# Router by token halves, with column-group products and split residual seeds, in a one-core encoder block with a mixture of experts

## Chip, cores and metric

One of the eight cores of a Trainium2 chip runs the whole program in one launch. The metric is the device time of one execution in microseconds (us), given as the median of several executions. Engines are called by the profile's names: PE (matrix products), PEld (its weight loads), DVE (vector), ACT (scalar and table functions), POOL, and SP, which here only issues DMAs.

## The reference, cut to what matters

An encoder layer over 256 tokens of width 1024: three mixing branches, a gated sum, an output projection with a residual, then a hierarchical mixture of 16 experts, and a final norm. The change touches the output projection, the norm after it, the router and the gathering of tokens for the first group of experts.

```python
x = x + (g_ret * y_ret + g_na * y_na + g_xa * y_xa) @ w_out[l]
x = x + _hierarchical_moe(_rmsnorm(x, g_ffn[l]), w_router_group[l], ...)

# in _hierarchical_moe, t = (256, 1024) normed tokens
grp_p = softmax(t @ w_rg + b_rg)                  # 4 groups
grp_w, grp_idx = top_k(grp_p, 1)
exp_logits = (t @ w_re + b_re).reshape(-1, 4, 4)  # 4 experts in each group
in_grp = exp_logits of the chosen group
top_w, top_idx = top_k(softmax(in_grp), 2)        # 2 of the 4
top_w = top_w / sum(top_w) * grp_w
for g in range(4):
    a, u = t @ w_gate[g], t @ w_up[g]             # 4 experts, width 512
    out += (silu(a) * u * combine[:, g]) @ w_down[g]
```

## The kernel before, in words

Up to the mixed branch outputs the program is ordered by a planner. From the third output of the last branch on, it runs under `manual_schedule()`: every engine executes in the order in which the Python code emits, so the order of the calls is the order on each queue.

**The tail before the experts.** `wout(q, pts)` multiplies a quarter (two blocks of 128 rows) of `w_out`, split in a high and a low part, with the mixed tokens `m_hi`, `m_lo`: 6 products of 128x512 for each of the two token halves `a` (128 tokens each). Four quarters fill the column half n=0 (into `p0`), four more n=1 (into `p1`). `x1_sum(n, a)` (L889) adds the residual on DVE; `x1_sq` (L893) takes the sum of squares on ACT; `x1_T` (L898) transposes four 128x128 blocks on PE, `x1_ev` (L901) copies them to SBUF on ACT; `logits(n, a)` (L906) is four products with the transposed token block as the stationary operand and the router's weights `wr` (32 columns, 20 of them used) as the moving one. Each such fp32 product is two passes on PE, and the profile counts passes. `x1_rstd(a)` (L957, L958) gives the norm's factor `r2`, with a power on POOL. `normed_hi` (L985, ACT) and `normed_lo` (L989, DVE) write the normed tokens, split in two parts. `seed` (L912) puts x1 itself into the four accumulators `acc` by a product with the identity, so that the experts' outputs are added on top.

**Routing.** `route(a)` (L1017 on) is a chain of eleven steps of small DVE instructions, from the logits with factor and bias (L1018) over two maxima with their indices to the mask `msk` (L1010). The chains of the two halves are interleaved on DVE. The products at L1060 with a triangular and an all-ones matrix count for each token its place within its expert; L1073 adds that to `posm`, `counts` (L1077) takes the largest count, and `select(0)` (L1114) compares `posm` with 0..63, which gives the 0/1 matrices `pd` (tile X) that gather tokens into 64 slots for each of the 4 experts of group 0. `gather(pd, lead=True)` (L1129) multiplies the normed high parts with `pd` (16 products of 128x256), then the low parts (16 more), and the evictions at L1152 (ACT) and L1156 (DVE) write `xg`.

**Experts.** For each of 8 pairs of experts: gate and up (`gate_up`, L1197), down (`down`, L1216), and the scatter back into `acc` (L1254). In these products the stationary operand has 64 columns, and two column groups of PE (outputs on partitions 0 to 63 and 64 to 127) are written by products in turn. L1169 and L1176 (`place`) prepare the scatter.

**Loads of the expert weights.** `plan` is a list of 96 loads of 1 MB each (gate and up as two DMAs of 512 KB, down as one of 1 MB) in the order of their use. `fetch(tag)` (issues at L152, on SP's queue) takes the next load of the list into a buffer that has come free; SP waits there until the buffer's last reader is done. Counted from 0, the loads 0 to 11 are issued up to 291 us. Loads 12 and 13 go into the buffers of the w_out quarters 0 and 1 of n=1 (in tile h), load 14 into A0 (the mixed tokens of rows 0 to 511), 15 and 16 into the buffers of quarters 2 and 3, 17 into E0 (mixed tokens of rows 512 to 1023), 18 and 19 into T0 and T1, whose space is freed with the temporary pools after the last logits. From load 20 on, each goes into a buffer that the experts themselves give back: load 20 goes into B after the first `gate_up` quarter. The list and the buffers are as many after the change as before.

**PSUM.** Four banks of pool `psa` (tile pj) hold `p0`, `p1`, then transposes, then `acc`; four of `psc` (tile b) hold the logits, transposes, counts and gathers.

Of the kernel before, what the change touches and what calls it, by code (L numbers as in the profile page):

```python
# [9 lines left out]
F32 = mybir.dt.float32  # L10
# [20 lines left out]
def hybrid_encoder_kernel(  # L31
# [162 lines left out]
    def pj(shape):  # L194
        return psa.tile(shape, F32, tag="pj", name=nm("pj"))
# [677 lines left out]

    def wout(q, pts):
        w = halves.pop(0)
        for a in range(2):
            ts = slice(a * P, (a + 1) * P)
            for k in range(2):
                kk = 2 * q + k
                PE.matmul(pts[a], m_hi[kk // 4][:, kk % 4, ts], w[k][0], start=kk == 0, stop=False)  # L880
                PE.matmul(pts[a], m_hi[kk // 4][:, kk % 4, ts], w[k][1], start=False, stop=False)
                PE.matmul(pts[a], m_lo[kk // 4][:, kk % 4, ts], w[k][0], start=False, stop=kk == KT - 1)
        if not parts:
            hl_tags.remove(w[2])
            fetch(w[2])

# [16 lines left out]
    def logits(n, a):  # L903
        for j in range(4):
            k = 4 * n + j
            PE.matmul(rlog[a], x1T[n][:, j, a * P : (a + 1) * P], wr[:, k], start=k == 0, stop=k == KT - 1)  # L906

    acc = [[None, None], [None, None]]

    def seed(base, a, n):  # L910
        acc[a][n] = acc[a][n] or pj([P, 512])
        PE.matmul(acc[a][n], ident, base[:, a, n * 512 : n * 512 + 512], start=True, stop=False)  # L912

    x1 = slot("C1", [P, 2, D])
    p0 = [pj([P, 512]) for _ in range(2)]
    for q in range(4):
        if q < 2:
            mt = mixed_T(1, q)
        wout(q, p0)
        if q < 2:  # L920
            mixed(1, q, mt)
        feed()
    psx.close()
# [4 lines left out]

    rlog = [bank([P, 32]) for _ in range(2)]
    p1 = [pj([P, 512]) for _ in range(2)]  # L930
    xt = [bank([P, 4, P]) for _ in range(2)]
    x1T[0] = tmp([P, 4, 256])
    x1_sum(0, 0, p0)
    x1_sum(0, 1, p0)
    x1_sq(0, 0)
    x1_sq(0, 1)
    wout(0, p1)
    feed()
    wout(1, p1)
    fetch("A0")  # L940
    x1_T(0, 0, xt[0])
    x1_T(0, 1, xt[1])
    feed()
    x1_ev(0, 0, xt[0])
    x1_ev(0, 1, xt[1])
    wout(2, p1)
    logits(0, 0)
    logits(0, 1)
    feed()
    wout(3, p1)  # L950
    xt = [pj([P, 4, P]) for _ in range(2)]
    x1T[1] = tmp([P, 4, 256])
    r2 = cp.tile([P, 2], F32, name="r2")

    def x1_rstd(a):
        v = tiny(1, tag="var")
        V.scalar_tensor_tensor(v, ss4[:, 2 * a : 2 * a + 1], 1e-6, ss4[:, 2 * a + 1 : 2 * a + 2], op0=ALU.add, op1=ALU.add)  # L957
        G.tensor_tensor(r2[:, a : a + 1], v, nhalf[:, :1], op=ALU.pow)  # L958

    x1_sum(1, 0, p1)  # L960
    fetch("E0")
    x1_T(1, 0, xt[0])
    x1_sq(1, 0)
    x1_ev(1, 0, xt[0])
    x1_sum(1, 1, p1)
    x1_rstd(0)
    x1_T(1, 1, xt[1])
    logits(1, 0)
    x1_sq(1, 1)
    x1_ev(1, 1, xt[1])  # L970
    logits(1, 1)
    x1_rstd(1)
    tx.close()
    tpx.close()
    fp = ctx.enter_context(tc.tile_pool(name="fp", bufs=1))
    for tag in ("T0", "T1"):
        home[tag] = fp
        fetch(tag)

# [12 lines left out]

    for a in range(2):
        for n in range(2):
            normed_hi(a, n)
            seed(x1, a, n)
    show("x1", x1)
    gval = cp.tile([P, 2, 8], F32, name="gval")
# [18 lines left out]
    def route(a):  # L1017
        V.scalar_tensor_tensor(lgt[:, a, 0:20], rlog[a][:, :20], r2[:, a : a + 1], rb, op0=ALU.mult, op1=ALU.add)  # L1018
        yield
        V.max(gval[:, a], lgt[:, a, 16:24])  # L1020
        yield
        V.max_index(gidx[:, a], gval[:, a], lgt[:, a, 16:24])
        yield
        V.tensor_tensor(ohg[:, a], io4, gidx[:, a, 0:1].to_broadcast([P, 4]), op=ALU.is_equal)
        yield
        V.tensor_tensor(
            sel[:, a],
            lgt[:, a, 0:16].rearrange("p (g e) -> p g e", g=4),
            ohg[:, a].unsqueeze(2).to_broadcast([P, 4, 4]),
            op=ALU.mult,  # L1030
        )
        yield
        V.tensor_reduce(pad[:, a, 0:4], sel[:, a].rearrange("p g e -> p e g"), axis=AX.X, op=ALU.add)
        yield
        V.max(eval_[:, a], pad[:, a])
        yield
        V.max_index(eidx[:, a], eval_[:, a], pad[:, a])
        yield
        for i in range(2):
            V.tensor_tensor(oh[:, i, a], io4, eidx[:, a, i : i + 1].to_broadcast([P, 4]), op=ALU.is_equal)  # L1040
        yield
        V.tensor_add(m4[:, a], oh[:, 0, a], oh[:, 1, a])
        yield
        spread(msk, m4, a)
        yield

    rt = [route(a) for a in range(2)]
    for i in range(16):
        if i < 11:
            next(rt[0])  # L1050
        if i >= 5:
            next(rt[1])
    pp = bank([P, 3, 16])
    for o, pieces in (
        (pp[:, 0], ((tri, 0),)),
        (pp[:, 1], ((tri, 1), (ones, 0))),
        (pp[:, 2], ((ones, 0), (ones, 1))),
    ):
        for i, (l, a) in enumerate(pieces):
            PE.matmul(o, l, msk[:, a], start=i == 0, stop=i == len(pieces) - 1)  # L1060
    posm = cp.tile([P, 2, 16], F32, name="posm")
    V.tensor_scalar(posm, msk, 1e6, -1e6, op0=ALU.mult, op1=ALU.add)
    gneg = tiny(2, tag="gneg")
    V.tensor_scalar_mul(gneg, gval[:, :, 0], -1.0)
    gsum = tiny(2, tag="gsum")
    for a in range(2):
        gex = tiny(4, tag="gex")
        A.activation(gex, lgt[:, a, 16:20], AF.Exp, bias=gneg[:, a : a + 1], accum_out=gsum[:, a : a + 1])
    e21 = tiny(2, tag="e21")
    V.tensor_sub(e21, eval_[:, :, 1], eval_[:, :, 0])  # L1070
    A.activation(e21, e21, AF.Exp)
    A.activation(warm, e21[:, 0:1], AF.Silu)
    V.tensor_add(posm, posm, pp[:, 0:2])  # L1073
    cmax = tiny(1, tag="cmax")

    def counts():
        V.tensor_reduce(cmax, pp[:, 2], axis=AX.X, op=ALU.max)  # L1077

    def weights():
# [28 lines left out]

    counts()

    def select(g):
        pd = slot("X", [P, 2, 4, SLOTS], F32R)
        for a in range(2):
            V.tensor_tensor(  # L1114
                pd[:, a],
                posm[:, a, 4 * g : 4 * g + 4].unsqueeze(2).to_broadcast([P, 4, SLOTS]),
                iota.unsqueeze(1).to_broadcast([P, 4, SLOTS]),
                op=ALU.is_equal,
            )
        return pd  # L1120

    def gather(pd, lead=False):
        pts = [bank([P, 2, 256]) for _ in range(4)]

        def part(u, x, first):
            for j in range(2):
                ks = slice((2 * u + j) * P, (2 * u + j + 1) * P)
                for a in range(2):
                    PE.matmul(  # L1129
                        pts[u][:, j],  # L1130
                        x[:, a, ks],
                        pd[:, a].rearrange("p e s -> p (e s)"),
                        start=first and j + a == 0,
                        stop=not first and j + a == 2,
                    )

        if lead:
            for u in range(4):
                part(u, x1_hi, True)
            for n in range(2):  # L1140
                for a in range(2):
                    normed_lo(a, n)
        xg = slot("C1", [P, KT, 4, SLOTS])
        for u in range(4):
            pt = pts[u]
            if not lead:
                part(u, x1_hi, True)
            part(u, x1_lo, False)
            if u % 2:
# [12 lines left out]
        return xg  # L1162
# [128 lines left out]

    def experts(pd, first, lead=False):
        st = {}
# [17 lines left out]

        xg = gather(pd, lead)
        for p in range(NP):
            tail = p == NP - 1
# [31 lines left out]

    pd0 = select(0)
    experts(pd0, weights, True)
    run.close()

# [81 lines left out]
```

## Time and profile before

| | us |
|---|---|
| median of 3 executions | 544.58 (544.51 to 544.82) |
| the profiled execution, whole | 544.12 |
| its span, first to last instruction | 542.2 |
| PE busy | 527.7 (97% of the span) |
| DVE busy | 263.6 (49%) |
| ACT busy | 228.6 (42%) |
| DMA queue of the loads | 158.80 MB, 80.4% of 16 engines |

The profile page gives busy time by engine, slices of the span, DMA queues, groups of instructions by source line (L906 is line 906 of the kernel), and the DMA issues. The timeline lists instructions in order of time; neighbours of one kind are merged (x8), and the duration is then that of the merged stretch. The duration of a PE row runs to a modelled end, and passes overlap in the array: the rate of a stretch is read from the distance of the starts. In brackets stands the idle time of the engine before the row and what ended it.

### The profile page before, as it was taken

The numbers are of one execution on the slowest core, as the hardware profiler recorded it, in microseconds if no ns is written. First come the engines' busy times: TensorE is split into PE (matmuls) and PEld (weight loads), VectorE is DVE, ScalarE is ACT, GpSimd is POOL, SyncE is SP. The second block draws the span as 40 slices with busy tenths as digits, with TensorE's granted clock in tenths as the row PEclk, the third lists the DMA queues.
The fourth block names the chain that finished last, engine by engine and source line by source line (L and its number), as shares of the span: only waits on it lengthen the run. The fifth ranks groups of instructions, "written<-read, shape, count | busy, mean of one in ns | idle before, by whom it ended". The sixth has DMA issues, their size and how long they took to land. (4 is left out here: it accounts for less than half of the span.)

```text
span 542.2 us, 7482 instructions
## 1 busy us (share of the span) xinstructions
PE 527.7 (97%) x2912; PEld 360.0 (66%) x2912; DVE 263.6 (49%) x461; ACT 228.6 (42%) x378; POOL 18.2 (3%) x21
## 2 busy tenths in 40 slices
PE   8999999999999999999999999999999999999992
PEld 7999899976778888888888863353435343534340
DVE  6688898985657768384566161030112111210122
ACT  7684567697754464544435251111111111111123
POOL 0014000040000000000000000000000000000000
PEclk9999999999999999999999999999999999999997
DMA  8997878044446698739983789999999999999962
GB/s 302 390 328 224 244 142 257 14 158 152 154 147 208 239 328 279 280 107 403 351 315 143 289 332 342 414 406 417 406 415 409 410 413 407 417 405 418 406 245 82
DMA packets 89815, 159.91 MB, mean 295 GB/s; under 512 B 13104, under 2 KB 27824, under 8 KB 89776
## 3 DMA queue, kind: packets, MB, share of 16 engines
q1 hardware_dynamic: 89056, 158.80, 80.4%
q10 hardware_dynamic: 720, 0.58, 0.3%
q8 instruction: 25, 0.41, 0.3%
q14 instruction: 14, 0.11, 0.1%
HBM read 158.32 MB, written 1.05 MB: 294 GB/s over the span
## 5 line engine op out<-in xcount | busy, mean ns | idle before, releaser
L129 DVE TENSOR_TENSOR h<-r,h 128x1024 fp32r<-128x1024 f32 x58 | 70.1, 1222 | 28.4 <-ACT h L128 28.1
L128 ACT CAST h<-r 128x1024 fp32r<-128x1024 f32 x58 | 59.9, 1047 | 17.7 <-PE pj L308 11.5
L306 PE MATMUL pj<-h,A 128*128 128x512 f32 x160 | 63.2, 395 | 0.0
L308 PE MATMUL pj<-h,A 128*128 128x512 f32 x160 | 62.6, 391 | 0.0
L307 PE MATMUL pj<-h,A 128*128 128x512 f32 x160 | 62.5, 391 | 0.0
L1205 DVE TENSOR_TENSOR gs<-gs,b 64x512 f32<-64x512 f32 x16 | 11.0, 691 | 87.1 <-ACT gs L1204 87.1
L288 PE MATMUL pj<-A,h 128*128 128x256 f32 x160 | 45.7, 286 | 0.0
L290 PE MATMUL pj<-A,h 128*128 128x256 f32 x160 | 45.5, 284 | 0.0
L289 PE MATMUL pj<-A,h 128*128 128x256 f32 x160 | 45.3, 283 | 0.0
L306 PEld LDWEIGHTS pj<-h,A 128*128 128x128 f32 x160 | 30.0, 188 | 7.0 <-issue 0.8
L308 PEld LDWEIGHTS pj<-h,A 128*128 128x128 f32 x160 | 30.1, 188 | 6.6 <-issue 0.4
L307 PEld LDWEIGHTS pj<-h,A 128*128 128x128 f32 x160 | 30.1, 188 | 6.3 <-DVE h L129 0.4
L1236 DVE SCALAR_TENSOR_TENSOR os<-b,c,os 128x512 fp32r<-128x512 f32 x16 | 12.0, 751 | 41.9 <-ACT os L1235 41.0
L1204 ACT ACTIVATE gs<-b 64x512 f32<-64x512 f32 x16 | 9.4, 589 | 51.8 <-PE b L1197 51.8
L288 PEld LDWEIGHTS pj<-A,h 128*128 128x128 f32 x160 | 30.7, 192 | 0.1
L290 PEld LDWEIGHTS pj<-A,h 128*128 128x128 f32 x160 | 30.7, 192 | 0.1
L289 PEld LDWEIGHTS pj<-A,h 128*128 128x128 f32 x160 | 30.7, 192 | 0.1
L129 DVE TENSOR_TENSOR h<-G,h 128x1024 fp32r<-128x1024 f32 x18 | 24.4, 1361 | 11.3 <-ACT h L128 10.8
L1235 ACT ACTIVATE os<-b,c 128x512 fp32r<-128x512 f32 x16 | 11.0, 687 | 40.6 <-PE b L1216 39.7
L1197 PE MATMUL b<-h,C 128*64 128x512 f32 x104 | 24.0, 592 | 0.0
L128 ACT CAST h<-G 128x1024 fp32r<-128x1024 f32 x18 | 18.8, 1050 | 10.3 <-PE pj L308 9.0
L1216 PE MATMUL b<-h,hh 128*64 128x512 f32 x64 | 21.3, 592 | 0.0
(328 smaller groups left out, 1029.4 us busy)
## 6 DMA issues: line engine op xcount, KB each, us to landing
r<-in_w_in_dram SPq DMA_DIRECT2D x20, 1024.0 KB, 5.5
h<-in_w_exp_down_dram SPq DMA_DIRECT2D x10, 1024.0 KB, 11.5
h<-in_w_exp_gate_dram SPq DMA_DIRECT2D x13, 512.0 KB, 11.0
h<-in_w_exp_up_dram SPq DMA_DIRECT2D x13, 512.0 KB, 11.2
r<-in_w_exp_down_dram SPq DMA_DIRECT2D x6, 1024.0 KB, 11.6
A<-in_w_exp_down_dram SPq DMA_DIRECT2D x5, 1024.0 KB, 11.4
r<-in_w_exp_gate_dram SPq DMA_DIRECT2D x9, 512.0 KB, 10.2
r<-in_w_exp_up_dram SPq DMA_DIRECT2D x9, 512.0 KB, 10.3
```

The costliest lines, as they stand in the source:

```text
L128: pin(A.copy(hi, part))
L129: pin(V.tensor_sub(lo, part, hi.bitcast(F32)))
L288: PE.matmul(pt, whi[:, cs], thi[:, k], start=k == 0, stop=False)
L289: PE.matmul(pt, whi[:, cs], tlo[:, k], start=False, stop=False)
L290: PE.matmul(pt, wlo[:, cs], thi[:, k], start=False, stop=k == kn - 1)
L306: PE.matmul(pts[a], thi[:, kk, ts], whi, start=first, stop=False)
L307: PE.matmul(pts[a], thi[:, kk, ts], wlo, start=False, stop=False)
L308: PE.matmul(pts[a], tlo[:, kk, ts], whi, start=False, stop=last)
L1197: PE.matmul(pt[c * 64 : c * 64 + 64], xg[:, k, p % 2 * 2 + i], w[:, 2 * c + j], start=k == 0, stop=k == KT - 1)
L1205: V.tensor_mul(gs[i * 64 : i * 64 + 64], gs[64:128], pt[64:128])
L1216: PE.matmul(pts[n][i * 64 : i * 64 + 64], hh[:, 2 * u + k], ws[i][1][:, k, ns], start=u + k == 0, stop=u + k == 2)
L1236: V.scalar_tensor_tensor(o[:, 1], pt, c, o[:, 0].bitcast(F32), op0=ALU.mult, op1=ALU.subtract)
```

## The change

The output projection's second column half and the router run by token halves: all four `wout` quarters of n=1 for half a=0 come first, then those of a=1 with half 0's router between them. The calls for n=0 stay as they were.

The router's logits swap their operands: `wr[:, k]` (32 columns) becomes the stationary operand and the transposed tokens the moving one (128 columns), and the four products of one call write four different groups of 32 partitions, so each of the four sums two of the eight blocks. `bound(a)` adds the four partial sums up and turns them back: ACT copies the 128x128 result to SBUF, and one fp32 product with `four` (four stacked 32x32 identities) writes `rlog[a]`.

The seeds go straight into the banks `p0`, `p1` of the projection. They are issued one by one among the router's steps, each as two products of 256 columns, the last one in two pieces. `route` yields twice instead of after each step, and is run for half 0, then for half 1. Counts, `posm` and `pd` are made by halves (`settled`, `chosen`), and the gather by `part` calls: half 0's tokens for the first three of four banks before half 1's route, the rest after it. The power factor of half 1 comes after half 0's route on DVE. Logits, counts and gather share the four `psc` banks `lead`. The table load for Silu moves behind the evictions of the first gather, whose engines are swapped (ACT now takes banks 0 and 2). The `fetch` calls keep their order; those for quarters 1 to 3, A0 and E0 follow half 1's use.

The diff, cut to its core:

```diff
-    def wout(q, pts):
-        w = halves.pop(0)
-        for a in range(2): ...
+    def wout(q, pts, w, a, ks=(0, 1)):
+    def used(w):
+        hl_tags.remove(w[2])
+        fetch(w[2])
...
     def logits(n, a):
         for j in range(4):
             k = 4 * n + j
-            PE.matmul(rlog[a], x1T[n][:, j, a * P : (a + 1) * P], wr[:, k], start=k == 0, stop=k == KT - 1)
+            PE.matmul(sheaf[a][32 * j : 32 * j + 32], wr[:, k],
+                x1T[n][:, j, a * P : (a + 1) * P], start=not n, stop=bool(n))
+    def bound(a):
+        A.copy(sheaves[:, a], sheaf[a])
+        PE.matmul(rlog[a], sheaves[:, a], four, start=True, stop=True)
...
+    lead = [bank([P, 512]) for _ in range(4)]
+    spare = lead[3]
+    acc = [[p0[a], p1[a]] for a in range(2)]
+    def seed(base, a, n, hs=(0, 1)):
+        for h in hs: ...   # 256 columns each
...
+    for a in range(2):
+        wout(0, p1, ws[0], a)
+    used(ws[0])
+    wout(1, p1, ws[1], 0)
+    for a in range(2):
+        x1_T(0, a, xt[a])
+        x1_ev(0, a, xt[a])
+    wout(2, p1, ws[2], 0)
+    wout(3, p1, ws[3], 0)
+    for a in range(2):
+        logits(0, a)
+    x1_sum(1, 0, p1)
+    x1_sq(1, 0)
+    x1_rstd(0)
+    wout(1, p1, ws[1], 1)
+    used(ws[1])
+    fetch("A0")
+    x1_T(1, 0, xt[2])
+    x1_ev(1, 0, xt[2])
+    for n in range(2):
+        normed_hi(0, n)
+        normed_lo(0, n)
+    wout(2, p1, ws[2], 1)
+    used(ws[2])
+    logits(1, 0)
+    wout(3, p1, ws[3], 1, (0,))
+    bound(0)
+    wout(3, p1, ws[3], 1, (1,))
+    used(ws[3])
+    fetch("E0")
+    rt = [route(a) for a in range(2)]
+    next(rt[0])
+    x1_sum(1, 1, p1)
+    x1_sq(1, 1)
+    next(rt[0])
+    x1_rstd(1)
+    seed(x1, 0, 0)
+    x1_T(1, 1, xt[1])
+    x1_ev(1, 1, xt[1])
+    seed(x1, 1, 0)
+    logits(1, 1)
+    PE.matmul(pp[0], tri, msk[:, 0], start=True, stop=True)
+    pd0 = slot("X", [P, 2, 4, SLOTS], F32R)
+    settled(0)
+    chosen(pd0, 0, 0)
+    bound(1)
...            # pools closed, fetch T0, T1
+    for u in range(3):
+        for x in (x1_hi, x1_lo):
+            part(lead[u], u, x, pd0, 0, x is x1_hi, False)
+    for n in range(2):
+        normed_hi(1, n)
+    for _ in range(2):
+        next(rt[1])
+    seed(x1, 0, 1)
...            # pp[1], pp[2]
+    settled(1)
+    counts()
+    chosen(pd0, 0, 1)
+    seed(x1, 1, 1, (0,))
+    part(spare, 3, x1_hi, pd0, 0, True, False)
+    part(spare, 3, x1_lo, pd0, 0, False, False)
+    for u in range(4):
+        part(lead[u], u, x1_hi, pd0, 1, False, False)
...            # gneg, e21
+    for n in range(2):
+        normed_lo(1, n)
+    for u in range(4):
+        part(lead[u], u, x1_lo, pd0, 1, False, True)
+    seed(x1, 1, 1, (1,))
```

## Rows read from the trace of the kernel before

**Rows 1.** Windows: busy us (instructions) of each engine, PE clock, DMA share, GB/s.

```profile
323.30:527.60 204.30, 204.30 (x1061) 84.27 (x1060) 33.59 (x69) 34.98 (x65) 0.00 (x0) 1.00 1.01 395
```

**Rows 2.** Timeline of PE before the experts: start us, us, engine line op out<-in xcount.

```profile
297.56 0.39 PE L880 MATMUL pj<-h,A 128*128 128x512 f32 x1
...
303.00 1.03 PE L898 MATMUL b<-ident,C 128*128 128x128 f32 x8
...
306.62 1.87 PE L906 MATMUL b<-wr,t 128*128 128x32 f32 x16
308.32 0.47 PE L880 MATMUL pj<-h,E 128*128 128x512 f32 x1
...
312.12 0.66 PE L898 MATMUL pj<-ident,C 128*128 128x128 f32 x4 [0.35 <-DVE C L889]
312.62 2.01 PE L906 MATMUL b<-wr,t 128*128 128x32 f32 x16
314.46 3.68 PE L912 MATMUL pj<-C,ident 128*128 128x512 f32 x8
317.98 0.20 PE L1060 MATMUL b<-msk,tri 128*128 128x16 bf16 x2
...
319.08 0.81 PE L1129 MATMUL b<-X,C 128*128 128x256 f32 x3 [0.83 <-DVE X L1114]
```

**Rows 3.** Timeline of PE, from the low gathers into the experts.

```profile
321.29 2.08 PE L1129 MATMUL b<-X,E 128*128 128x256 f32 x16
323.30 1.94 PE L1197 MATMUL b<-B,C 128*64 128x512 f32 x8
...
333.75 0.44 PE L1169 MATMUL b<-ident,X 128*128 128x128 f32 x2
334.12 0.40 PE L1176 MATMUL b<-cmb,X 128*64 128x1 f32 x8
334.37 1.06 PE L1197 MATMUL b<-r,C 128*64 128x512 f32 x4
```

**Rows 4.** Timeline of DVE in the router.

```profile
311.38 0.69 DVE L889 TENSOR_TENSOR C<-pj,t 128x512 f32<-128x512 f32 x1 [0.70 <-PE pj L882]
...
314.96 0.23 DVE L1018 SCALAR_TENSOR_TENSOR lgt<-b,r,rb 128x20 f32<-128x20 f32 x1
...
317.29 0.17 DVE L1010 TENSOR_TENSOR msk<-ohg,m 128x16 bf16<-128x16 f32 x1
...
318.29 0.19 DVE L1073 TENSOR_TENSOR posm<-posm,b 128x32 f32<-128x32 f32 x1 [0.47 <-PE b L1060]
...
318.51 0.76 DVE L1114 TENSOR_TENSOR X<-posm,iota 128x256 fp32r<-128x256 f32 x2
319.19 2.73 DVE L989 SCALAR_TENSOR_TENSOR E<-C,r,C 128x512 fp32r<-128x512 f32 x4
```

**Rows 5.** Timelines of ACT and POOL in the router.

```profile
312.21 0.55 POOL L958 TENSOR_TENSOR r<-var,nhalf 128x1 f32<-128x1 f32 x1 [124.05 <-DVE var L957]
...
312.92 0.57 ACT L901 COPY t<-pj 128x512 f32<-128x512 f32 x1
```

**Rows 6.** Timeline of SP's queue: issues of loads 12 to 14, 20 and 87.

```profile
300.51 3.05 SPq L152 DMA_DIRECT2D h<-in_w_exp_down_dram  x2
303.61 0.47 SPq L152 DMA_DIRECT2D A<-in_w_exp_down_dram  x1
...
325.69 0.47 SPq L152 DMA_DIRECT2D B<-in_w_exp_up_dram  x1
...
487.65 0.63 SPq L152 DMA_DIRECT2D r<-in_w_exp_down_dram  x1
```

**Rows 7.** DMA issues of loads 20 (second DMA) and 87: us to landing.

```profile
B<-in_w_exp_up_dram SPq DMA_DIRECT2D x1, 512.0 KB, 5.4
...
r<-in_w_exp_down_dram SPq DMA_DIRECT2D x1, 1024.0 KB, 15.0
```

**Rows 8.** Timeline of PEld: first use of load 87.

```profile
505.35 0.14 PEld L1216 LDWEIGHTS b<-r,hh 128*64 128x64 f32 x2 [0.28 <-issue]
```

More of the change, by code (lines that the diff above doesn't have):

```diff
@@ L872, in hybrid_encoder_kernel @@
     x1T = {}
-    def wout(q, pts):
-        w = halves.pop(0)
[L876 to L885, printed above, removed]
+    def wout(q, pts, w, a, ks=(0, 1)):
+        ts = slice(a * P, (a + 1) * P)
+        for k in ks:
+            kk = 2 * q + k
+            PE.matmul(pts[a], m_hi[kk // 4][:, kk % 4, ts], w[k][0], start=kk == 0, stop=False)
+            PE.matmul(pts[a], m_hi[kk // 4][:, kk % 4, ts], w[k][1], start=False, stop=False)
+            PE.matmul(pts[a], m_lo[kk // 4][:, kk % 4, ts], w[k][0], start=False, stop=kk == KT - 1)
+    def used(w):
+        hl_tags.remove(w[2])
+        fetch(w[2])
     def x1_sum(n, a, pts):
@@ L905, in logits @@
             k = 4 * n + j
-            PE.matmul(rlog[a], x1T[n][:, j, a * P : (a + 1) * P], wr[:, k], start=k == 0, stop=k == KT - 1)
[L908 to L912, printed above, removed]
+            PE.matmul(
+                sheaf[a][32 * j : 32 * j + 32],
+                wr[:, k],
+                x1T[n][:, j, a * P : (a + 1) * P],
+                start=not n,
+                stop=bool(n),
+            )
+    def bound(a):
+        A.copy(sheaves[:, a], sheaf[a])
+        PE.matmul(rlog[a], sheaves[:, a], four, start=True, stop=True)
     x1 = slot("C1", [P, 2, D])
@@ L918, in hybrid_encoder_kernel @@
             mt = mixed_T(1, q)
-        wout(q, p0)
+        w = halves.pop(0)
+        for a in range(2):
+            wout(q, p0, w, a)
         if q < 2:
             mixed(1, q, mt)
+        if not parts:
+            used(w)
         feed()
@@ L927, in bank @@
         return psc.tile(shape, F32, tag="b", name=nm("b"))
-    rlog = [bank([P, 32]) for _ in range(2)]
-    p1 = [pj([P, 512]) for _ in range(2)]
[L931 to L952, printed above, removed]
+    lead = [bank([P, 512]) for _ in range(4)]
+    spare = lead[3]
+    rlog = [lead[0][:, 32:64], spare[:, 32:64]]
+    pp = [lead[0][:, 0:16], spare[:, 64:80], spare[:, 80:96]]
+    sheaf = [b[:, 128:256] for b in (lead[0], spare)]
+    sheaves = cp.tile([P, 2, P], F32, name="sheaves")
+    four = cp.tile([P, 32], F32, name="four")
+    for g in range(4):
+        gs = slice(32 * g, 32 * g + 32)
+        A.copy(four[gs], ident[gs, gs])
+    xt = [b.rearrange("p (j t) -> p j t", j=4) for b in lead]
+    p1 = [pj([P, 512]) for _ in range(2)]
+    acc = [[p0[a], p1[a]] for a in range(2)]
+    def seed(base, a, n, hs=(0, 1)):
+        for h in hs:
+            cs = slice(h * 256, h * 256 + 256)
+            PE.matmul(acc[a][n][:, cs], ident, base[:, a, n * 512 + h * 256 : n * 512 + h * 256 + 256], start=not h, stop=False)
+    for n in range(2):
+        x1T[n] = tmp([P, 4, 256])
     r2 = cp.tile([P, 2], F32, name="r2")
@@ L958, in x1_rstd @@
         G.tensor_tensor(r2[:, a : a + 1], v, nhalf[:, :1], op=ALU.pow)
[L960 to L978, printed above, removed]
     x1_hi = slot("C2", [P, 2, D], F32R)
@@ L991, in normed_lo @@
         )
[L993 to L997, printed above, removed]
     gval = cp.tile([P, 2, 8], F32, name="gval")
@@ L1018, in route @@
         V.scalar_tensor_tensor(lgt[:, a, 0:20], rlog[a][:, :20], r2[:, a : a + 1], rb, op0=ALU.mult, op1=ALU.add)
-        yield
         V.max(gval[:, a], lgt[:, a, 16:24])
-        yield
         V.max_index(gidx[:, a], gval[:, a], lgt[:, a, 16:24])
@@ L1024, in route @@
         V.tensor_tensor(ohg[:, a], io4, gidx[:, a, 0:1].to_broadcast([P, 4]), op=ALU.is_equal)
-        yield
         V.tensor_tensor(
@@ L1031, in route @@
         )
-        yield
         V.tensor_reduce(pad[:, a, 0:4], sel[:, a].rearrange("p g e -> p e g"), axis=AX.X, op=ALU.add)
-        yield
         V.max(eval_[:, a], pad[:, a])
-        yield
         V.max_index(eidx[:, a], eval_[:, a], pad[:, a])
-        yield
         for i in range(2):
             V.tensor_tensor(oh[:, i, a], io4, eidx[:, a, i : i + 1].to_broadcast([P, 4]), op=ALU.is_equal)
-        yield
         V.tensor_add(m4[:, a], oh[:, 0, a], oh[:, 1, a])
-        yield
         spread(msk, m4, a)
@@ L1045, in route @@
         yield
-    rt = [route(a) for a in range(2)]
[L1048 to L1058, printed above, removed]
-        for i, (l, a) in enumerate(pieces):
-            PE.matmul(o, l, msk[:, a], start=i == 0, stop=i == len(pieces) - 1)
-    posm = cp.tile([P, 2, 16], F32, name="posm")
@@ L1062, in hybrid_encoder_kernel, with settled, chosen @@
-    V.tensor_scalar(posm, msk, 1e6, -1e6, op0=ALU.mult, op1=ALU.add)
+    posm = cp.tile([P, 2, 16], F32, name="posm")
+    V.tensor_scalar_add(iota, iota, 1e6)
+    def settled(a):
+        V.scalar_tensor_tensor(posm[:, a], msk[:, a], 1e6, pp[a], op0=ALU.mult, op1=ALU.add)
+    def chosen(pd, g, a):
+        V.tensor_tensor(
+            pd[:, a],
+            posm[:, a, 4 * g : 4 * g + 4].unsqueeze(2).to_broadcast([P, 4, SLOTS]),
+            iota.unsqueeze(1).to_broadcast([P, 4, SLOTS]),
+            op=ALU.is_equal,
+        )
@@ new lines, in part, with counts @@
+    def part(pt, u, x, pd, a, first, last):
+        pt = pt.rearrange("p (j c) -> p j c", j=2)
+        for j in range(2):
+            k = 2 * u + j
+            PE.matmul(
+                pt[:, j],
+                x[:, a, k * P : (k + 1) * P],
+                pd[:, a].rearrange("p e s -> p (e s)"),
+                start=first and not j,
+                stop=last and j == 1,
+            )
+    cmax = tiny(1, tag="cmax")
+    def counts():
+        V.tensor_reduce(cmax, pp[2], axis=AX.X, op=ALU.max)
@@ new lines, in hybrid_encoder_kernel @@
+    for a in range(2):
+        x1_sum(0, a, p0)
+        x1_sq(0, a)
+    ws = [halves.pop(0)]
+    for a in range(2):
+        wout(0, p1, ws[0], a)
+    used(ws[0])
+    feed()
+    ws += halves
+    wout(1, p1, ws[1], 0)
+    for a in range(2):
+        x1_T(0, a, xt[a])
+        x1_ev(0, a, xt[a])
+    wout(2, p1, ws[2], 0)
+    wout(3, p1, ws[3], 0)
+    for a in range(2):
+        logits(0, a)
[4 more added lines that the diff above has]
+    used(ws[1])
@@ new lines, in hybrid_encoder_kernel @@
+    seed(x1, 1, 0)
[5 more added lines that the diff above has]
+    bound(1)
+    tx.close()
+    tpx.close()
+    fp = ctx.enter_context(tc.tile_pool(name="fp", bufs=1))
+    for tag in ("T0", "T1"):
+        home[tag] = fp
+        fetch(tag)
+    for u in range(3):
[3 more added lines that the diff above has]
+        normed_hi(1, n)
@@ new lines, in hybrid_encoder_kernel @@
+    for _ in range(2):
+        next(rt[1])
+    seed(x1, 0, 1)
+    for o, pieces in ((pp[1], ((tri, 1), (ones, 0))), (pp[2], ((ones, 0), (ones, 1)))):
+        for i, (l, a) in enumerate(pieces):
+            PE.matmul(o, l, msk[:, a], start=i == 0, stop=i == 1)
+    settled(1)
[6 more added lines that the diff above has]
+        part(lead[u], u, x1_hi, pd0, 1, False, False)
@@ L1063, in hybrid_encoder_kernel @@
     gneg = tiny(2, tag="gneg")
     V.tensor_scalar_mul(gneg, gval[:, :, 0], -1.0)
+    e21 = tiny(2, tag="e21")
+    V.tensor_sub(e21, eval_[:, :, 1], eval_[:, :, 0])
+    for n in range(2):
+        normed_lo(1, n)
+    for u in range(4):
+        part(lead[u], u, x1_lo, pd0, 1, False, True)
+    seed(x1, 1, 1, (1,))
     gsum = tiny(2, tag="gsum")
@@ L1068, in hybrid_encoder_kernel @@
         A.activation(gex, lgt[:, a, 16:20], AF.Exp, bias=gneg[:, a : a + 1], accum_out=gsum[:, a : a + 1])
-    e21 = tiny(2, tag="e21")
-    V.tensor_sub(e21, eval_[:, :, 1], eval_[:, :, 0])
     A.activation(e21, e21, AF.Exp)
[L1072 to L1077, printed above, removed]
+    show("x1", x1)
     def weights():
@@ L1107, in wide @@
         return fp.tile(shape, dt, tag="os", name=nm("os"), bufs=2)
-    counts()
     def select(g):
@@ L1113, in select, with gather @@
         for a in range(2):
[L1114 to L1119, printed above, removed]
-        return pd
[L1122 to L1142, printed above, removed]
+            chosen(pd, g, a)
+        return pd
+    def gather(pd, pts=None):
+        done = pts
+        pts = pts or [bank([P, 512]) for _ in range(4)]
         xg = slot("C1", [P, KT, 4, SLOTS])
@@ L1145, in gather @@
             pt = pts[u]
[L1146 to L1149, printed above, removed]
+            for x in () if done else (x1_hi, x1_lo):
+                for a in range(2):
+                    part(pt, u, x, pd, a, x is x1_hi and a == 0, x is x1_lo and a == 1)
+            pt = pt.rearrange("p (j c) -> p j c", j=2)
+            if bool(u % 2) != bool(done):
                 for j in range(2):
@@ L1290, in finish, with experts @@
                 (nc.sync, nc.scalar)[a].dma_start(out[0, a * P : (a + 1) * P, n * 512 : n * 512 + 512], o)
-    def experts(pd, first, lead=False):
+    def experts(pd, first, lead=None):
         st = {}
@@ L1312, in experts @@
         xg = gather(pd, lead)
+        if lead:
+            A.activation(warm, e21[:, 0:1], AF.Silu)
         for p in range(NP):
@@ L1345, in experts @@
         finish(1)
-    pd0 = select(0)
-    experts(pd0, weights, True)
+    experts(pd0, weights, lead)
     run.close()
```

## Prediction

> **What bounds the kernel now.** [...] Load 87 is issued at 487.65 and lands 15.0 us later, at 502.7; PE first uses it at 505.35 [rows 6 to 8]. Followed the same way through all 96 loads, the margin is nowhere smaller than these 2.6 us. PE therefore sets the end, and whatever brings it to the experts earlier shortens the whole, as long as the loads follow within that margin.
>
> The change lies in the stretch before. I read it in PE's timeline, from the first w_out product of the column half n=1 (297.56) to the first expert product (323.30): 25.74 us [rows 2, 3]. The 24 products from 297.56 to 303.00 give 0.227 us for one of 128x512; the 8 transposes have one pass of 0.11 us each; the router's 16 passes take 1.70 us the first time (306.62 to 308.32) and 1.84 the second; the four seeds take 3.52 (314.46 to 317.98); the gathers 0.12 each (2.01 for 16, with the change to the experts' products behind them) [rows 2, 3]. Sum of the work: 48 x 0.227 + 16 x 0.11 + 3.54 + 3.52 + five counting products, 0.13, + 32 x 0.12 = 10.9 + 1.75 + 3.54 + 3.52 + 0.13 + 3.84 = 23.7. The remaining 2.0 us are waits: about 0.5 for the residual sum ahead of the last transposes, nearly 1.0 for `posm` and `pd` ahead of the gather (317.98 + 0.13 to 319.08), 0.3 inside its first products, where X of the second half is still being written, and 0.2 of restarts [rows 2, 4].
>
> **Part by part.** *The w_out products by token halves.* The same 48 products, no cost in PE time. What they move is the order of buffer release, below.
>
> *Logits.* 32 passes that cost 3.54 go. In their place come 16 fp32 products with 32 stationary columns, in four column groups, four to a call. The trace of before shows no product on 32 columns, so the price is bounded. From below: products on two column groups do overlap; eight passes of 512 columns on two groups in turn take 1.94 us, while the seeds' eight on the full width take 3.68 [rows 2, 3]. Eight full ones at 0.44 make 0.11 for a pass of 128 columns, and if four groups run side by side a call costs two passes in turn, 0.22. The eight passes of L1176, on two groups, take 0.25 (334.12 to 334.37) [rows 3]. From above: the four products run one after another, as eight passes of 0.11, 0.88, about half the old 1.70. I take 0.25 a call, since both rows of column groups show overlap from the first pair on: 4 x 0.25 = 1.0.
>
> *Switches of the array's form.* PE goes three times from full width to column groups and back. From L1169's two transposes (333.75 + 2 x 0.11) to 334.12 it is 0.15; behind the 16 gathers it is at most 0.09 (2.01 less 16 x 0.12) [rows 3]. Six switches at 0.12 are 0.7 (0 to 0.9).
>
> The trace shows a gap at each switch, at most 0.15. [...]
>
> *Adding up (`bound`).* Two products of two passes, 4 x 0.11 = 0.44. Each is preceded by an ACT copy of 128 columns, which I put at 0.3 against 0.57 for 512 [rows 5]. The four small copies for `four` lie on ACT where it idles. *Seeds:* as many columns, 3.52, in other places. *Gather and counts:* as many, 3.84 and 0.13.
>
> So work falls from 23.7 to 10.9 + 1.75 + 1.0 + 0.7 + 0.44 + 3.52 + 0.13 + 3.84 = 22.3, by 1.4.
>
> **Waits after the change.** I walk the new order with the rows' prices. PE finishes the last w_out product at 297.56 + 10.9 + twelve transposes 1.3 + three logits calls 0.75 + four switches 0.5 + the first `bound` 0.2 + restarts 0.1 = 311.3. Half 0's norm factor and high and low parts are done by then on ACT, POOL and DVE, behind w_out products of half 1. Then:
> - The residual sum of half 1 ends near 312.2 (0.4 from the last product's start, 0.69 on DVE [rows 4]). Seed (0,0), 0.88 long, covers PE to 312.2: wait 0.1. Transposes to 312.7.
> - Before, the copy started 0.85 after the residual sum's end (311.38 + 0.69 to 312.92), with the square between, and took 0.57 [rows 4, 5]: it ends at 313.6. Seed (1,0) covers PE to 313.6. Logits of half 1 to about 314.1.
> - Meanwhile half 0 is routed. A chain takes 2.50 (314.96 to 317.29 + 0.17 [rows 4]); what is left of it after its first three steps takes about 1.75, so the mask is there at 314.0, just before PE wants it.
> - The first counting product is issued at 314.1. From there to `posm` it took 0.31, `posm` 0.19, X 0.42 for one half, and 0.15 more to the first gather (318.51 + 0.42 to 319.08) [rows 2, 4]: first gather at 315.2. In between lie the sheaf copy and `bound(1)`. Waits 0.45 and 0.4, the largest of the new order.
> - 12 gathers of half 0 and seed (0,1) take PE to 317.5. On DVE half 1's chain starts at 315.05 and, alone, takes 2.50: mask at 317.55. Wait 0.1.
> - Counting, `posm`, `counts` until 318.3; half a seed covers to 318.15: wait 0.2. Four gathers, then X of half 1 at 318.85; eight high gathers to 319.85. The low parts of half 1 start on DVE after the two short steps at 319.0, at 0.68 each [rows 4]: the second is ready at 320.4, where PE waits 0.1. Last gather 320.9, half a seed, one switch: first expert product at 321.5.
>
> Evictions: bank 0 is complete at 320.3, ACT has 0.9 us of work on it, and PE comes at 321.5. The waits add up to 1.4 where they were 2.0 (restarts included in both). Gain 1.4 + 0.4 to 0.6, at the walk 323.30 - 321.5 = **1.8 us**. With no wait at all it would be 3.1; with the two long waits doubled and the copies late, 0.4.
>
> **The loads.** Loads 13 and 14 were issued at about 303.2 and 303.6 [rows 6]. Now their buffers come free after the half-1 products of quarter 1, at 307.5. SP's queue is in order, so 15 to 19 stand behind them; but their own releases (309.3, 311.5, 312, and 314.3 for the pools) are within 3 us of before, and the list is never empty from there on. Load 13 then lands some 4.7 after its issue, 312.3, and the rest follow at about 2.57 us a load, the mean spacing in the full stream from load 20 at 331.1 (325.69 + 5.4) to load 87 at 502.7, 171.6 / 67 [rows 6, 7]. Load 20 lands at 330.3 instead of 331.1: before, the engines ran dry between 19 and 20, as no buffer was free, and that hole takes up the lateness. The stream is 0.8 earlier, PE 1.8, and the margin at load 87 goes from 2.6 to about 1.6. Nothing waits.
>
> **Rivals.**
> 1. *A wait takes the place of the one removed.* The new order hangs on single results: the sheaf copies stand on ACT behind `normed_hi` and the copy of the transposes, with 0.1 us to spare ahead of `bound(0)`. If the waits double, from 1.4 to 2.8, gain 0.4: 544.2. For it: half 1's route no longer overlaps half 0's on DVE. Against it: PE has seeds and gathers to fill in.
> 2. *The products do not run side by side.* Then a call costs 0.88: 4 x 0.63 = 2.5 more, of which the chains absorb some 0.4. Gain -0.3: 544.9. Against it: rows 3 show overlap of two groups.
> 3. *Slower: every change of column group costs a switch.* 16 products at 0.25 more for leaving and entering, and one after another: 4.0 - 0.7 + 2.5 - 0.4 = 5.4 more than the walk, 3.6 slower, 548.2. It turns slower than before once a product costs 1.8 / 16 = 0.11 more than I take. Against it: the L1176 passes change groups within 0.25 us for eight [rows 3].
> 4. *The loads become the bound.* If the stretch from load 13 to 20 goes at 2.8 us a load, load 20 lands at 331.9, 0.8 late; the margin of 2.6 then allows a gain of 1.8 and hardly more, and with 2.9 only 1.1: 543.5.
>
> **How the numbers follow.** The profiled execution took 544.12, 0.46 less than the median of the runs and 1.9 more than its span. The gain is counted in its own time (544.12 to 542.3) and taken off the median: 544.58 - 1.8 = 542.8. Chances: forecast (gain 1.1 to 3.1) 0.60; rival 1 0.20; rival 2 0.08; rival 3 0.07; rival 4 0.05. 0.2% of this kernel is 1.1 us, about what a measurement can tell from no change. Faster: 0.60 + 0.05 = 0.65; within 0.2%: rivals 1 and 2, 0.28; slower 0.07. The range goes from no wait left (541.5) to rival 1 with a little more (544.5) and leaves out rivals 2 and 3.
>
> **What would show it.** PE's first expert product near 321.5; logits calls of 0.25 us, not 0.9; gaps of about 0.1 at their ends; PE idle by about 0.4 on either side of `bound(1)` and nowhere longer; load 87 still landing ahead of its use. I am wrong if the logits calls take 0.8, if a wait of over 0.6 stands ahead of `bound` or the gather, or if PE waits on a load late in the experts.

## The result: slower, and where the time went

The changed kernel takes 549.51 us (median, 549.19 to 550.18) against 544.59 for the kernel before: ratio 1.0092, interval 1.0082 to 1.0102. Forecast were 542.8 and faster. Its profiled execution took 550.18, the longest of its six, and its span is 548.3; before, the span was 542.2. The stretches below are of that one execution and add up to 6.1 us, where the medians differ by 4.9.

I cut both spans at the same two products: the first w_out product of the column half n=1 (before 297.56 [rows 2], after 299.27) and the first expert product (before 323.30 [rows 3], after 323.95). PE's timeline of the changed kernel, from the first cut to the experts (start us, us, engine line op out<-in xcount, idle before <- releaser):

```profile
299.27 0.39 PE L878 MATMUL pj<-h,A 128*128 128x512 f32 x1
...
307.07 0.65 PE L905 MATMUL b<-t,wr 128*32 128x128 f32 x16
307.65 0.50 PE L878 MATMUL pj<-h,A 128*128 128x512 f32 x1
...
311.10 0.43 PE L905 MATMUL b<-t,wr 128*32 128x128 f32 x8
311.45 0.50 PE L878 MATMUL pj<-h,E 128*128 128x512 f32 x1
...
312.25 0.30 PE L915 MATMUL b<-four,sheaves 128*128 128x32 f32 x2
312.39 0.48 PE L878 MATMUL pj<-h,E 128*128 128x512 f32 x1
...
313.17 1.02 PE L953 MATMUL pj<-C,ident 128*128 128x256 f32 x4
...
316.37 0.41 PE L915 MATMUL b<-four,sheaves 128*128 128x32 f32 x2 [0.27 <-ACT sheaves L914]
316.82 0.51 PE L1035 MATMUL b<-X,C 128*128 128x256 f32 x2
...
322.53 0.59 PE L953 MATMUL pj<-C,ident 128*128 128x256 f32 x2
323.95 0.65 PE L1234 MATMUL b<-B,C 128*64 128x512 f32 x2 [0.83 <-ACT C L1189]
```

- Before the first cut: +1.71 us.
- The router, which the change is about: 323.95 - 299.27 = 24.68 against 25.74, **-1.06**.
- From the first expert product to the end: 548.3 - 323.95 = 224.35 against 542.2 - 323.30 = 218.9, **+5.45**.

The change does what it says, and loses five times as much in a stage that it does not touch. There, PE waits for loads. Counted from the first expert product, the first 914 of PE's 1074 passes (before: up to 501.9 us) start in both kernels at the same distance, to 0.03 us; from then on PE falls behind by 5.3 us, all of it at four waits for loads (0.4, 2.0, 2.2 and 0.7). So the products themselves have not become slower. The waits of the changed kernel, grouped by what ended them (line waited for: us in total, times, longest), are these; they are shorter than what PE loses at them, as they count from the modelled end of a product. The kernel before has no row with a load of the experts:

```profile
PE b L1253 <- DMA r<-in_w_exp_down_dram: 2.9, 2, 1.5
...
PE b L1234 <- ACT C L1189: 0.8, 1, 0.8
PE b L1264 <- DMA A<-in_w_exp_down_dram: 0.5, 1, 0.5
...
PE b L1253 <- DMA A<-in_w_exp_down_dram: 0.2, 1, 0.2
```

PE's own timeline late in the experts shows two of them, 1.42 and 1.47; the second is for load 87, the one of [rows 6 to 8]:

```profile
505.44 0.64 PE L1253 MATMUL b<-r,hh 128*64 128x512 f32 x1 [1.42 <-DMA r<-in_w_exp_down_dram]
...
508.06 1.03 PE L1253 MATMUL b<-r,hh 128*64 128x512 f32 x4
510.56 0.65 PE L1253 MATMUL b<-r,hh 128*64 128x512 f32 x2 [1.47 <-DMA r<-in_w_exp_down_dram]
```

Load 87 lands at 510.5, 2.0 after PE wants it; before, it was there 2.6 early. Load 20, issued at 325.92 and landed with its second DMA 7.4 us after 326.33, is there at 333.7, so that the 67 loads between come 176.8 / 67 = 2.64 us apart; before, 2.56. The SP rows and the landings:

```profile
326.33 0.47 SPq L152 DMA_DIRECT2D B<-in_w_exp_up_dram  x1
```

```profile
B<-in_w_exp_up_dram SPq DMA_DIRECT2D x1, 512.0 KB, 7.4
...
r<-in_w_exp_down_dram SPq DMA_DIRECT2D x1, 1024.0 KB, 15.6
```

The stream is slower though the DMA engines are as full as ever. In the windows from 340 to 480 us (columns as in [rows 1]), the kernel before and then the one after have the same DMA share, 1.04, and the same clock, and differ in the last column, 411 against 397 GB/s:

```profile
340.00:480.00 140.00, 140.00 (x724) 59.39 (x722) 22.80 (x44) 23.77 (x44) 0.00 (x0) 1.00 1.04 411
```

```profile
340.00:480.00 140.00, 140.00 (x724) 59.40 (x722) 22.73 (x45) 23.75 (x44) 0.00 (x0) 1.00 1.04 397
```

Full engines that move less: each packet takes longer. Taken from the trace's DMA records between loads 22 and 95, a packet of 2 KB (one row of a gate or up load) takes 88.3 ns in place of 84.1, one of 4 KB (down) 162.9 in place of 159.0, and a load of gate and up 2.71 us in place of 2.55 (the median distance of two landings). That is some 4 ns a row on the mean, long or short. Single rows differ: of the 2 KB rows in the window above, 99% take 84 ns in the kernel before; in the changed kernel 23% still do, and the slowest 5% take 95 ns or more.

Which buffer a load fills decides it. In the changed kernel only loads into T0 and T1 still go at 84.0 ns and 2.50 us; in the kernel before, T0 and T1 were the slow ones, 85.1 ns and 2.65 us. That points at their place in SBUF. The change adds two tiles to the pool of constants:

```diff
+    sheaves = cp.tile([P, 2, P], F32, name="sheaves")
+    four = cp.tile([P, 32], F32, name="four")
```

They take 1024 and 128 bytes of each partition, together 1152, four and a half times 256: everything allocated behind them moves by that. The load buffers of the pool start at multiples of 256 before and 128 past one after; T0 and T1 the other way round.

### The profile page after: what moved, and what is told of

Read it like the earlier page. It is cut to its first block, busy times and chain, and to the rows that moved or that the text cites. A ratio compares the mean times of both kernels' runs of the same rounds, so it can differ in the third digit from the quotient of the medians.

```text
span 548.3 us, 7511 instructions
## 1 busy us (share of the span) xinstructions
PE 528.6 (96%) x2924; PEld 359.9 (66%) x2924; DVE 264.8 (48%) x462; ACT 229.9 (42%) x384; POOL 18.2 (3%) x21
```

## Experiments

**The address put right.** Theory A: rows that don't start at a multiple of 256 bytes are what costs 5 us. Rivals: the releases that the change makes later starve the queue (B), or the larger program or the place in HBM (C).

```diff
-    four = cp.tile([P, 32], F32, name="four")
+    four = cp.tile([P, 64], F32, name="four")[:, :32]
```

> The changed kernel with one constant tile 128 bytes longer per partition, so that every buffer of the weight loads starts at a multiple of 256 bytes in SBUF again, as before the change (the change's two new tiles, 1152 bytes, had moved them to 128 past such a multiple). Theory A, the start addresses slow the loads: loads of gate and up land every 2.55 us again instead of 2.70, PE waits for no load, the early 1.7 us go too, and only the router's 1.06 us stay: 543.5. Theory B, the later release of the buffers of loads 13 to 17 starves the stream: nothing changes, 549.5. Theory C, the larger program or its place in HBM slows the loads: 549.5, with 2.70 us a load.

Measured: 543.39 us, ratio to before 0.9985 (0.9975 to 0.9994), that is 6.1 us less than the changed kernel by the medians, 5.8 by the two ratios, for 128 unused bytes. The window is back at the rate of before:

```profile
340.00:480.00 140.00, 140.00 (x724) 59.39 (x722) 22.80 (x44) 23.77 (x44) 0.00 (x0) 1.00 1.04 411
```

The stretch before the first cut comes back too (297.79), load 87 has 2.0 us of margin, and no wait for a load of the experts is left. The router takes 24.68, as without the bytes (297.79 to 322.47). B and C fall: releases, instructions and program are those of the changed kernel.

**The address put wrong, nothing else.** The kernel before with an unused tile, at four sizes; no instruction differs. First 128 bytes, which puts the buffers where the change put them:

```diff
+    cp.tile([P, 32], F32, name="unused")
```

> The kernel before with one unused tile of 128 bytes per partition, which moves all buffers by 128 bytes and changes no instruction. Theory A: gate and up loads every 2.70 us, load 87 about 4.8 us later against a margin of 2.6, and 1.7 us lost in the first 50 us: 548 to 549. Theories B and C: 544.6, as no release and no instruction changes.

Measured: 549.85 us, ratio 1.0113 (1.0091 to 1.0135). Its window is that of the changed kernel, at 397 GB/s:

```profile
340.00:480.00 140.00, 140.00 (x724) 59.41 (x722) 22.71 (x45) 23.75 (x44) 0.00 (x0) 1.00 1.04 397
```

Loads 85 and 87 come 1.8 and 2.0 us late, the second as much as in the changed kernel. So the whole loss appears without any part of the change's work. (The 1.7 us expected for the first 50 us were 0.65 here: the first w_out product comes at 298.20.) Then 64 bytes (`[P, 16]`):

> The kernel before, buffers moved by 64 bytes. If it is the start at a multiple of 256 that counts: slower loads, 2.6 to 2.8 us for gate and up, time 547 to 550. If only an odd multiple of 128 is bad, or only a start below 64: 2.55 us and 544.6.

Measured: 551.24 us (one run). T0 and T1 lie at 192 past a multiple here, and are slow too, 2.71 us. Then 256 bytes (`[P, 64]`), which moves every buffer and keeps it at a multiple of 256:

> The kernel before with an unused tile of 256 bytes per partition in the pool of constants, as in e2_shift128 and e4_shift64, but keeping every load buffer at a multiple of 256 bytes. If the place within 256 bytes is what makes the loads slower: 544.6, loads 2.55 us apart. If any move of the buffers does it, or it takes a multiple of 512 bytes: near 549.8, 2.7 us apart.

Measured: 544.55 us, ratio 1.0001 (0.9991 to 1.0011). Moving the buffers by 256 bytes cost nothing (rows at 84.1 ns, as before); the place within 256 bytes is what costs, and 256 past a multiple of 512 is as good as 0. Last 32 bytes (`[P, 8]`):

> The kernel before with an unused tile of 32 bytes per partition: every load buffer of the pool lies 32 bytes past a multiple of 256. Theory X (a row that does not start at a multiple of 256 bytes costs one fixed extra, whatever the distance): as at 64 and 128 bytes, rows of 2 KB at 88 ns, loads 2.71 us apart, time 549.5 to 550.5. Theory Y (the extra grows with the distance, as 4.3 ns at 128 bytes would make 1.1 at 32): rows at 85.1 ns, loads near 2.60 us apart, and with 2.6 us of margin for 67 loads the time only 0 to 1 us longer, 544.6 to 545.5. [...]

Measured: 552.11 us (two runs), rows at 88.1 ns: theory X. My own expectation of 549.5 to 550.5 for it was too low. T0 and T1 are off as well here, but that can be no more than a part: of what the profiled execution (553.09) takes more than the kernel before, 3.2 us stand ahead of the first w_out product (300.72), more than in any other run, and why is open. From the trace's DMA records, by where the pool's buffers and T0/T1 start (bytes past a multiple of 256):

```
                        pool / T    2 KB row, ns   load apart, us   GB/s      median
                                    pool    T      pool    T        340:480   us
before                  0 / 128     84.1   85.1    2.55   2.65      411       544.59
after                   128 / 0     88.3   84.0    2.71   2.50      397       549.51
after, 128 bytes more   0 / 128     84.1   85.2    2.56   2.67      411       543.39
before + 128 bytes      128 / 0     88.3   84.0    2.71   2.50      397       549.85
before + 64 bytes       64 / 192    88.2   88.4    2.71   2.71      395       551.24
before + 256 bytes      0 / 128     84.1   85.3    2.57   2.67      411       544.55
before + 32 bytes       32 / 160    88.1   88.4    2.71   2.71      395       552.11
```

In the pool's buffers the mean cost does not grow with the distance: 32, 64 and 128 bytes all make a row 4 ns longer. T0 and T1 do not follow so plainly: at 128 past, with aligned loads around them in the queue, their rows take 85.1 and not 88.3; at 160 and 192, with all other loads off too, 88.4. No run separates the distance from the neighbours there. The price is measured here on the side that is written: only the place in SBUF was moved. Theory Y, 85.1 ns a row at 32 bytes, falls by the 88.1 measured there. Nor is it a fixed price for each row, as single rows take anything from 84 to 98 ns. What makes up the 4 ns is not shown by these runs.

**The last wait taken away.** In the changed kernel PE waits 0.83 for `xg` ahead of the experts. ACT's and DVE's timelines show what their evictions waited for, the last half seed (L953):

```profile
323.16 1.57 ACT L1189 ACTIVATE C<-b,gt 128x256 f32<-128x256 f32 x4 [1.92 <-PE pj L953]
```

```profile
323.16 1.29 DVE L1193 TENSOR_TENSOR C<-b,gt 128x512 f32<-128x512 f32 x2 [1.33 <-PE pj L953]
```

`xg` lies in slot C1, the place of `x1`, and that seed still reads `x1`. Both engines had been idle for more than a microsecond by then. On top of the 128 bytes, the seed is moved ahead of the low gathers:

```diff
+    seed(x1, 1, 1, (1,))
     for u in range(4):
         part(lead[u], u, x1_lo, pd0, 1, False, True)
-    seed(x1, 1, 1, (1,))
```

> As the first kernel of this call, and the last half seed goes ahead of the four last pairs of gathers instead of behind them. The evictions of the first gather write the buffer from which that seed reads. If this is what held them: ACT's first eviction starts right after bank 0 is complete, the idle 0.8 us of PE ahead of the first expert product go, and the time is 1.0 us below the first kernel's, 542.5. If ACT or DVE itself was late: no difference to the first kernel, 543.5.

Measured: 542.39 us, ratio 0.9964 (0.995 to 0.9978), faster than both kernels. The wait is 0.22, and the router takes 322.11 - 298.06 = 24.05, 1.69 less than before and 0.63 less than with the seed in its old place. The medians of these two differ by 1.0; the 0.4 beyond the 0.63 is within the intervals. PE's timeline, then ACT's, whose first eviction now follows the gathers:

```profile
320.35 0.60 PE L953 MATMUL pj<-C,ident 128*128 128x256 f32 x2
320.59 1.30 PE L1035 MATMUL b<-X,E 128*128 128x256 f32 x8
322.11 1.94 PE L1234 MATMUL b<-B,C 128*64 128x512 f32 x8 [0.22 <-ACT C L1189]
```

```profile
321.21 1.57 ACT L1189 ACTIVATE C<-b,gt 128x256 f32<-128x256 f32 x4 [1.21 <-PE b L1035]
```

**The same seed, but with the loads slow.** The changed kernel with that move and without the 128 bytes tells which of the two engines sets the end there.

> The changed kernel with its addresses as they are (load buffers 128 bytes past a multiple of 256), and the last half seed (1,1) moved ahead of the low gathers, as in e3_pad_seed: PE can come to the experts about 0.65 us earlier. Theory A (loads landing 2.71 us apart set the end): PE's earlier start only lengthens its later waits for loads, time unchanged, 549.5 (549.2 to 550.2). Rival P (PE still sets the end and its products have become slower for some other cause): the time falls by what PE gains, to 548.5 to 548.9.

Measured: 549.27 us, ratio 1.0093 (1.0076 to 1.0109). The interval is too wide to tell theory A from rival P by the time alone; the traces tell them apart. PE's first 914 passes in the experts keep the distances of the kernel before here too, so its products are no slower, and rival P falls. The router takes 24.05 here too (298.44 to 322.49), 0.63 less; 0.3 of that comes back in longer waits for loads, and from the first cut to the end it is 248.7 in place of 249.0. The other comparison is plainer: the kernel before with 128 bytes has the old router (25.74, 1.06 more than the changed kernel) and takes 249.0 as well. With slow loads little or nothing of the router's gain reaches the end.

**What the column groups are worth.** The best kernel with the logits as they were, straight into `rlog`; all else in the new order.

```diff
-            PE.matmul(sheaf[a][32 * j : 32 * j + 32], wr[:, k], x1T[n][:, j, a * P : (a + 1) * P], start=not n, stop=bool(n))
+            PE.matmul(rlog[a], x1T[n][:, j, a * P : (a + 1) * P], wr[:, k], start=k == 0, stop=k == KT - 1)
...
-        A.copy(sheaves[:, a], sheaf[a])
-        PE.matmul(rlog[a], sheaves[:, a], four, start=True, stop=True)
+        pass
```

> e3_pad_seed with the router's products as in the kernel before (transposed rows stationary, 32 columns moving, straight into rlog; no column groups, no sheaf copy, no product against four), all else in the new order. It prices the column groups. If the price read from the changed kernel's trace holds (two calls side by side 0.65 with their switches against 1.70, and about even on the last call, which lies on the chain of half 1), it is 0.9 to 1.2 us slower than e3_pad_seed: 543.4, first expert product near 323.1. If the column groups were worth nothing and only the order and the seeds count: 542.4.

Measured: 544.06 us, ratio 0.9993 (0.9983 to 1.0002); the router takes 323.12 - 297.72 = 25.40. That is 1.35 us more than with column groups; by the two ratios (0.9993 less 0.9964 of 544.5) it is 1.6. Its logits:

```profile
305.42 1.87 PE L905 MATMUL b<-wr,t 128*128 128x32 f32 x16
307.13 0.47 PE L878 MATMUL pj<-h,A 128*128 128x512 f32 x1
```

Two calls take 1.71 from start to start, against 0.58 in the changed kernel. Of the router's gain of 1.69 the column groups, with their copy and the product against `four`, carry 1.35, the new order the rest.

**What filling the waits is worth.** The best kernel with its four seeds in one block ahead of the last low gathers.

```diff
-    seed(x1, 0, 0)
-    seed(x1, 1, 0)
-    seed(x1, 0, 1)
-    seed(x1, 1, 1, (0,))
-    seed(x1, 1, 1, (1,))
+    for a in range(2):
+        for n in range(2):
+            seed(x1, a, n)
```

> e3_pad_seed with the four seeds in one block just ahead of the last low gathers, and so in none of PE's waits; the same columns in all. If the seeds did fill waits (2.6 us of the 3.5 of them stand in waits for DVE and ACT), PE idles there and pays them again in the block: 2.5 to 3.2 us slower than e3_pad_seed, 545.2, first expert product near 325. If the waits would have been filled anyway, or the block hides behind the route of half 1: 542.4 to 543.

Measured: 545.65 us, ratio 1.0027 (1.0018 to 1.0037), 3.3 us more than with the seeds in the waits. PE waits 0.78 for the residual sum and 0.67 for its copy, where seeds stood:

```profile
312.77 0.66 PE L897 MATMUL b<-ident,C 128*128 128x128 f32 x4 [0.78 <-DVE C L888]
314.11 0.43 PE L905 MATMUL b<-t,wr 128*32 128x128 f32 x8 [0.67 <-ACT t L900]
```

Its profiled execution took 547.63, 2.0 over the median, and in its windows (PE clock third from the end) the clock falls:

```profile
310.00:315.00 5.00, 3.27 (x30) 2.03 (x22) 4.26 (x20) 2.01 (x6) 0.49 (x1) 1.00 1.02 417
315.00:320.00 5.00, 4.52 (x24) 4.16 (x25) 4.19 (x22) 2.10 (x7) 0.07 (x1) 0.59 1.03 408
```

From 310 to 315 the granted clock is 1.00 and PE, waiting, is busy for 3.27 us; from 315 to 320 the granted clock is 0.59, and PE's passes are longer: two of the gather's passes take 0.42 from start to start (316.42 to 316.84), against 0.24 in the changed kernel (317.17 to 317.41). The first expert product comes at 326.79 there. Of the ten executions two are that long (547.63 and 547.48), with mean clocks of 0.986 and 0.987; the other eight have 0.990 to 0.995. The median lies 2 us lower, so these 2 us are not the price of the block.

**T0 and T1 as well.** The best kernel with 128 unused bytes ahead of these two.

```diff
+    fp.tile([P, 32], F32, name="unused")
```

> e3_pad_seed with an unused tile of 128 bytes ahead of the two late buffers T0 and T1, so that these too start at a multiple of 256 bytes. Their loads come 2.5 us apart instead of 2.7; the margin of load 87 grows from 1.3 to about 2. Theory A (PE sets the end as long as no load is late): time as e3_pad_seed, 542.4. Rival: the loads still hold PE back somewhere, then it is faster by up to 0.8, 541.6.

Measured: 543.01 us, ratio 0.9971 (0.9958 to 0.9983), the same as without within the intervals. Rows into T take 84.0 ns, the margin of load 87 is 1.7 in place of 1.3 (I had expected 2). As no load is late in either, the faster loads brought nothing.

## Why the prediction was wrong, step by step

**The step that failed: "The loads".** It takes "about 2.57 us a load, the mean spacing in the full stream" from the kernel before, and ends with "Nothing waits". The spacing was no constant of the chip but of the buffers' addresses, and the diff, in two lines that allocate constants, moves these. It measured 2.64 on the mean, 2.71 for a gate and up load (the sum behind the 2.57, 171.6 / 67, gives 2.56). The 67 loads take 176.8 in place of 171.6, 5.2 us more on a margin of 2.6. Rival 4 named the right place ("the loads become the bound") with the wrong cause, a slow start between loads 13 and 20, and thereby a wrong size: a start can be late by a microsecond, a rate is paid on every load. It had 0.05. Its slow start did come, and harmed nothing by itself: see load 20 below.

The rows were there: loads into T0 and T1 at 2.65 us against 2.55 in the kernel before. I averaged over that difference instead of asking what sets these two buffers apart.

**Before the cut.** The prediction takes the 297.56 us ahead of the router as unchanged. They became 1.71 longer in the profiled execution. The w_in loads go into the same buffers: from 10 to 30 us 388 GB/s before and 360 after, 385 with the 128 bytes, which brings all but 0.2 of it back. That the address costs time here too is shown by the rate, in all runs: 358 to 360 GB/s with the pool off a multiple of 256, 385 to 389 on one. How much is not: with the same addresses the first cut comes 0.65 (kernel before with 128 bytes) and 0.88 us later (changed kernel, seed moved), and with aligned ones it varies by 0.5 (297.56 to 298.06).

**The second failed step: "Evictions: bank 0 is complete at 320.3 ... and PE comes at 321.5".** I asked when their bank was complete, not what they write over. They wait for the last half seed, which reads `x1`, and PE for them: a wait of 0.83 in place of none, and 24.05 in place of 24.68 when the seed stands earlier.

**What was right.** The walk through the router. With 1.71 taken off for the later start: end of the w_out products at 311.46 (predicted 311.3), first gather at 315.11 (315.2), last seed issued at 320.82 (320.9). Two logits calls take 0.58 with both switches, one 0.35: 0.23 a call (0.25 predicted) and 0.12 for the switch back; the switch in is about 0.1 (0.12 predicted for each). So the four products of a call do run side by side, and rivals 2 and 3 fall. `bound` takes 0.14 (0.22 predicted). Of the waits around `bound(1)`, 0.27 and 0.31 were measured for 0.45 and 0.4, and rival 1 (waits double) falls. Load 13 was issued at 309.4 and landed at 314.3, 1.71 taken off 307.7 and 312.6, for 307.5 and 312.3.

**Wrong without harm: load 20.** It should have been 0.8 earlier than before, at 330.3; with right addresses it landed at 331.9, 0.8 later. Load 13 landed at 312.5 there, so the seven loads between came 2.78 apart and not 2.57: the slow start of rival 4 ("2.8 us a load, load 20 lands at 331.9"), at its very figures. It set no end, as the 67 loads after it came 2.55 apart. That load 87 kept a margin of 2.0, near the 1.6 forecast, is luck, as the start of the stream was misjudged by 1.6. In the changed kernel, where the loads are the bound, a small part of the loss may be due to the later releases: from the first cut to the landing of load 20 it takes 34.4, against 34.0 in the kernel before with 128 bytes.

With both failed steps mended, the kernel takes 542.39 where 542.8 was forecast. But that takes two edits which the forecast kernel does not have. With the address alone put right it takes 543.39, and the router gains 1.06 of the 1.8 forecast. The router's work was priced well; one of its waits and the other thing that the diff changes were missed.

## What to carry to other kernels

A new tile moves every buffer behind it: where a stream of loads is full, work out the start of its buffers modulo 256 bytes before and after the edit, pad the new tile where it is not 0 (here 88.1 to 88.3 ns for a row of 2 KB in place of 84.1), and look in the trace for loads into one buffer that are slower than into the others. A stream with a margin of 2.6 us over 67 loads has 0.04 us a load to give, so a rate is to be checked before a delay. And where a step ends a wait, ask not only when its input is there but who still reads what it writes over.

## What the runs showed of the hardware that I had not expected

- In a full stream of rows written 32, 64 or 128 bytes past a multiple of 256, a row of 2 KB takes on the mean 88.1 to 88.3 ns, against 84.1 at a multiple; a row of 4 KB, measured at 128 past, takes 162.9 against 159.0. The stream falls from 411 GB/s to 397 (128 past) or 395 (32 and 64) while its DMA share stays at 1.04: the share doesn't show it, the rate does.
- Four products on 32 columns each, in four column groups, cost together 0.23 us (two calls 0.58, one 0.35); one alone, two passes of 0.11, would cost 0.22 by an estimate from the seeds of the kernel before (eight passes of 512 columns in 3.52, so 0.44 for one).
- Waits of 0.78 and 0.67 us in the router were followed, in the profiled execution of that kernel, by a granted clock of 0.59 over 5 us and a time 2.0 us over its median.
